# A third feed-forward by seven block products, and the forget-gate sums made one stage later

## The chip, the core and the metric

The kernel runs on one core of a Trainium2 chip. The core has a matrix engine (PE, with its weight loads shown apart as PEld), three engines for element-wise work (DVE, ACT, POOL) and a queue engine (SP) that issues most transfers; POOL issues some. The metric is the device time of one execution in microseconds, smaller is better. One execution was also recorded by the hardware profiler; all rows below come from that record.

## What is computed

The reference is one inference step of a two-layer decoder for 512 prompt tokens and 32 sample tokens (8 sequences of 4), all in float32. Each layer is: feed-forward, mixer, feed-forward. So there are four feed-forwards; the mixer of the first layer is a gated linear attention, that of the second a "forgetting" attention over shared keys and values.

```python
def swiglu(u, w_up, w_down):              # u: 544 x 1024, w_up: 1024 x 5632, w_down: 2816 x 1024
    a, b = jnp.split(u @ w_up, 2, axis=-1)
    return (jax.nn.silu(a) * b) @ w_down
...
logf = jax.nn.log_sigmoid((fl + b_f).astype(jnp.float32))      # one value per token and head
Ft = jnp.cumsum(logf.astype(jnp.float32), axis=1)              # enters the scores as Fi - Ft
...
h = h + 0.5 * gate * swiglu(u, ...)       # u = modulate(rmsnorm(h)), before and after each mixer
```

## The kernel before

**Layout.** Activations are kept transposed: 1024 features are 8 blocks (`NB`) of 128 partitions, the 544 tokens are two halves of 272 columns (`HALF`). Every float32 operand of a large product is split into a high and a low part (`halves`, lines 156 to 158: ACT rounds the high part, DVE subtracts to get the low part), and each product is three matmuls (`acc3`, lines 173 to 178). One feed-forward has 22 pairs (`NQ`): pair q is 128 columns of `a` and the 128 columns of `b` that gate them.

**The plain feed-forward, `ffn` (line 412).** For each pair and each half of the tokens, `up` makes `a` and `b`, each with 8 x 3 matmuls of 272 columns: 96 matmuls for a pair. `gated` (line 442 on) applies SiLU, multiplies and splits the result into `gh`, `gl`. `down` multiplies groups of pairs (2, 4, 4, 4, 4, 4) by the rows of `w_down` and `residual` (line 389) adds to `h`. In the last group all eight blocks of half 0 come first, then all eight of half 1; behind each half come `stats` and `make_u`, which make the input of the next stage. The plain form was used for three feed-forwards, named "00", "02" and "10"; their matmuls write tiles `pa`, `pb` and `pd`.

**The feed-forward by seven products, `ffn_seven` (line 508).** It was used for the last one alone, "12". The first three pairs are done plainly (`plain`). From the fourth pair on, the 2 x 2 blocks of the weights (a or b, by halves of the features) and of the inputs (by halves of the features and of the tokens) are multiplied by a scheme of seven block products in place of eight: 7 x 4 x 3 = 84 matmuls for a pair, which write tiles `p`. The block sums that it needs are extra work: of the inputs once (`inputs`, `last_input`: tiles `x`, `t`, `th`, `tl`), of the weights for each pair (`stage`: POOL, lines 611 to 618, and `halves`), of the results for each pair (`plus_ps`, line 643, and `low`, lines 648 and 649). `T3`, a block of the inputs, is written over a quarter of `uh`/`ul`. The 16 blocks of `down` of a round (rounds of 3, 3, 3, 3, 3, 3, 2, 2 pairs) are issued between the products of the next round; the last round, of two pairs, has half 0 first, then half 1.

**The forget gates' sums.** Four functions, `gate_logs`, `gate_turn`, `gate_tiles`, `gate_pages` (lines 1478 to 1523), turn the raw gate values `lf` into what the attention reads: rows of the DRAM scratch `klscr` and `qxscr`, and the tiles `nf` and `cum`. In the kernel before they are passed as `steps` to feed-forward "10" (line 1528), which issues one after every eleventh `gated`. Their tiles lie in a pool of their own, opened before "10".

**The attention, `fox` (line 1533 on).** After "10" come the projections `fq` (queries, two chunks of 512 columns, with `norm_heads` on DVE and POOL), then eight blocks `og_block` (`fg`, 48 matmuls each), whose weights come through `split_cols` and SP. The attention proper starts with the `cq` products and with `pair_loads(0)`, which reads `khscr`, `klscr` and `qxscr` back by POOL's queue into `kd`, `kl` and `qe`; the first score products `fs` need all three.

**The order of the work.** The kernel is written for a framework that schedules each engine's instructions itself: an instruction goes to its engine's queue when, by the framework's own estimate, its inputs and its tile's memory are there, and what stands earlier in the program goes first among those that are ready. So an instruction can run well ahead of the place where it is written. `gate_logs`, written behind the eleventh `gated` of "10", ran at the very start of "10"; the POOL memset of `gate_turn` and the 16 page loads of `gate_pages` ran before "10" began. Rings of buffers set limits: 4 raw weight tiles, 6 high, 6 low, 5 product banks.

Of the kernel before, what the change touches and what calls it, by code (L numbers as in the profile page):

```python
# [9 lines left out]
F32 = mybir.dt.float32  # L10
# [8 lines left out]
P = 128  # L19
# [80 lines left out]
def trunk_kernel(ctx: ExitStack, tc: tile.TileContext, a, out, dbg=None, stop=None):  # L100
# [407 lines left out]
    def ffn_seven(name, l, s, gate, after_half, steps=(), final=False, plain=3):  # L508
        wu = a["w_ffn_up"][l, s]
        wd = a["w_ffn_down"][l, s]  # L510
        steps = list(steps)
# [6 lines left out]
        with tc.tile_pool(name="ffn" + name, bufs=1) as fp:  # L518
            th, tl = ({i: fp.tile([P, H2, HA], F32R, name=f"t{x}{i}{name}") for i in (1, 2, 4)} for x in "hl")
            t3 = fp.tile([P, H2, HA], F32, name=f"t3{name}")  # L520
# [14 lines left out]

            def inputs():
                for k in range(H2):
                    x1, x2 = (tmp.tile([P, HA], F32, tag="nv", name=f"x{i}{name}_{k}", bufs=3)[:] for i in (1, 2))
                    x3 = t3[:, k]
# [6 lines left out]
                    minus(x3, x2, x3)  # L546
                    minus(x2, x2, x1)
                    halves(th[2][:, k], tl[2][:, k], x2)
                    x4 = tmp.tile([P, HA], F32, tag="nv", name=f"x4{name}_{k}", bufs=3)[:]
                    plus(x4, 1, 0, k)  # L550
                    minus(x4, x4, x2)
                    halves(th[4][:, k], tl[4][:, k], x4)
                    yield

            def last_input():
                S.copy(quarter(uh, 0, 1), t3[:])
                minus(quarter(ul, 0, 1), t3[:], quarter(uh, 0, 1).bitcast(F32))
# [8 lines left out]
            def g_tiles(q):  # L566
                gt[q] = (fp.tile([P, T], F32R, tag="gh", name=f"gh{name}_{q}", bufs=6),
                         fp.tile([P, T], F32R, tag="gl", name=f"gl{name}_{q}", bufs=6))
# [8 lines left out]
            def plain_up(q, half):  # L577
                t0, t1 = HALF[half]
# [3 lines left out]
                apply_u(pb, wt[q][1], half)  # L582
                g = tmp.tile([P, HA], F32, tag="sq", name=f"g{name}_{q}_{half}", bufs=3)
                S.activation(g[:], pa[:, 0:HA], AF.Silu)
                V.tensor_tensor(out=g[:], in0=g[:], in1=pb[:, 0:HA], op=ALU.mult)
                halves(gt[q][0][:, t0:t1], gt[q][1][:, t0:t1], g[:])

# [63 lines left out]
            def seven(q, between):  # L651
# [32 lines left out]
                if steps:  # L684
                    steps.pop(0)()
# [34 lines left out]
            for q in range(2):  # L720
                plain_weights(q)
            plain_up(0, 0)
            plain_up(1, 0)
            plain_up(0, 1)
# [21 lines left out]
            for r in range(1, len(rounds)):  # L746
                todo = blocks(r - 1)
                n, done = 7 * len(rounds[r]), [0]

                def between():  # L750
                    done[0] += 1
                    while len_out[0] < 2 * NB * done[0] // n:
                        next(todo)
                        len_out[0] += 1
                len_out = [0]
# [658 lines left out]
    gates = ExitStack()  # L1414
    gt_pool = gates.enter_context(tc.tile_pool(name="gate", bufs=1))
    lf = gt_pool.tile([P, 5, 16], F32, name="lf")
# [50 lines left out]
    le = gt_pool.tile([P, 5, 16], F32, name="le")  # L1467
    lt = gt_pool.tile([16, TP], F32, name="lt")
    rs = gt_pool.tile([16, TP], F32, name="rs")
    loc = gt_pool.tile([16, TP], F32, name="loc")  # L1470
    loc2 = gt_pool.tile([16, 2, TP], F32R, name="loc2")
    off = gt_pool.tile([16, 4, 4, 1], F32, name="off")
    off2 = gt_pool.tile([16, 2, 16], F32R, name="off2")
    gsm = gt_pool.tile([16, 16, P], F32, name="gsm")
    lp = gt_pool.tile([P, 2, 8, 16], F32, name="lp")
    lne = gt_pool.tile([32, 8, 16], F32, name="lne")

    def gate_logs():
        S.activation(le[:], lf[:], AF.Abs)
        S.activation(le[:], le[:], AF.Exp, scale=-1.0)  # L1480
        S.activation(le[:], le[:], AF.Ln, bias=1.0)
        V.tensor_scalar(out=lf[:], in0=lf[:], scalar1=0.0, scalar2=None, op0=ALU.min)
        V.tensor_tensor(out=lf[:], in0=lf[:], in1=le[:], op=ALU.subtract)
        G.dma_start(out=out[5][0].rearrange("(t p) h -> p t h", p=P), in_=lf[:, 0:4])
        G.dma_start(out=out[9].rearrange("b t h -> (b t) h"), in_=lf[0:32, 4])

    def gate_turn():
        ps = aux_bank("lfT")
        for t in range(4):
            PE.transpose(ps[0:16, t * P:(t + 1) * P], lf[:, t], ident)  # L1490
        V.tensor_copy(out=lt[:], in_=ps[0:16, :])
        G.memset(rs[:], 1.0)
        G.memset(rs[:].rearrange("p (c t) -> p c t", t=P)[:, :, 0:1], 0.0)
        V.tensor_tensor_scan(out=loc[:], data0=rs[:], data1=lt[:], initial=0.0, op0=ALU.mult, op1=ALU.add)

    def gate_tiles():
        hi, lo = loc2[:, 0], loc2[:, 1]
        halves(hi, lo, loc[:])
        SP.dma_start(out=klscr[:, 64:66], in_=loc2[:].bitcast(F32))
        V.memset(off[:], 0.0)  # L1500
        for qt in range(1, 4):
            for kt in range(qt - 1, -1, -1):
                V.tensor_tensor(out=off[:, kt, qt], in0=off[:, kt + 1, qt], in1=loc[:, kt * P + 127:kt * P + 128], op=ALU.subtract)
        halves(off2[:, 0], off2[:, 1], off[:].rearrange("p k q o -> p (k q o)"))
        for i in range(2):
            V.tensor_copy(out=gsm[:], in_=off2[:, i].bitcast(F32).unsqueeze(2).to_broadcast([16, 16, P]))
            SP.dma_start(out=qxscr[:, 2 + 4 * i:6 + 4 * i].rearrange("p k t -> p (k t)"), in_=gsm[:].rearrange("p a t -> p (a t)"))

    def gate_pages():
        for b in range(8):  # L1510
            for g in range(2):
                SP.dma_start(out=lp[:, g, b], in_=a["cache_logf"][bass.ds(pages[2 * b + g], 1)].rearrange("o t h -> t (o h)"))
        V.tensor_tensor(out=lne[:], in0=lf[0:32, 4].unsqueeze(1).to_broadcast([32, 8, 16]), in1=cst[0:32, C_SEQ:C_SEQ + 8].unsqueeze(2).to_broadcast([32, 8, 16]), op=ALU.mult)
        ps = aux_bank("nf")
        lpf = [lp[:, g].rearrange("p b h -> p (b h)") for g in range(2)]
        strict = cst[:, C_STRICT:C_STRICT + 128]
        PE.matmul(ps[:, 0:128], lhsT=lpf[0], rhs=strict, start=True, stop=False)
        PE.matmul(ps[:, 0:128], lhsT=lpf[1], rhs=ones, start=False, stop=True)
        PE.matmul(ps[:, 128:256], lhsT=lpf[1], rhs=strict, start=True, stop=True)
        PE.matmul(ps[:, 256:260], lhsT=lne[:].rearrange("p b h -> p (b h)"), rhs=cst[0:32, C_TRI4:C_TRI4 + 4], start=True, stop=True)  # L1520
        V.tensor_copy(out=nf[:, 0:256], in_=ps[:, 0:256])
        V.tensor_copy(out=cum[:], in_=ps[:, 256:260])
        V.tensor_scalar(out=nf[:, 256:260], in0=ps[:, 256:260], scalar1=-1.0, scalar2=None, op0=ALU.mult)
# [4 lines left out]
    ffn("10", 1, 0, mod(1, 0, 2), after("11", mod(1, 1, 0), mod(1, 1, 1)), [gate_logs, gate_turn, gate_tiles, gate_pages])  # L1528
    gates.close()
# [3 lines left out]
    def fox(after_half):  # L1533
        W = a["fox_w_qg"][0]
        with ExitStack() as es:
# [13 lines left out]
            with tc.tile_pool(name="foxq", bufs=1) as gp:  # L1549
# [293 lines left out]
```

## Time and profile before

| what | us |
|---|---|
| median of 3 runs | 2429.81 |
| fastest, slowest | 2422.88, 2434.22 |
| the profiled execution | 2429.69 |
| its span, first to last instruction | 2427.9 |
| feed-forward "10", first to last product | 1329.66 to 1733.00 |
| projections of the attention (`fq`, then `fg`) | 1734.81 to 1839.8 |
| feed-forward "12", first to last product | 2037.41 to 2419.95 |

Times in rows are microseconds from the start of the span. A row of the view by windows gives, for a stretch, each engine's busy time and the number of instructions that fall in it. A row of the view by lines gives a group of like instructions: line, engine, operation, out<-in, shape, count, then busy time and mean duration in ns, then the idle time of the engine before them and what ended it. Matmuls overlap each other, so that a matmul of "289 ns" does not cost the engine 289 ns; the cost of one is taken from how many start in a stretch that is full.

### The profile page before, as it was taken

To read this page: it belongs to the slowest core of one execution; us is meant where nothing else is said; L and a number is where in the kernel's file an instruction comes from. 1 tells how busy PE (TensorE), PEld (TensorE's weight loads), DVE (VectorE), ACT (ScalarE), POOL (GpSimd) and SP (SyncE) were. 2 spreads that over 40 slices of the span, in tenths; PEclk is the share of its full clock that TensorE was granted. 3 is DMA by queue.
4 is the path that set the end of the run, shared out by engine and by line. 5 is a ranking of instruction groups with operands and counts; after the bars stand their busy time and mean duration, and the time that the engine had idled before them with its cause. 6 is when DMAs were issued, how large, how long until landed. Compare 5 with 4: busy or idle time off the path is not lost.

```text
span 2427.9 us, 48518 instructions
## 1 busy us (share of the span) xinstructions
PE 2362.8 (97%) x19976; PEld 2215.4 (91%) x19976; DVE 1381.7 (57%) x3082; ACT 832.4 (34%) x1529; POOL 443.5 (18%) x574
## 2 busy tenths in 40 slices
PE   7999999998999999999999999999998899999999
PEld 6999999997979999999979999999896569999999
DVE  6343343548556453443585345344766666888887
ACT  3212222334534222221334323222435544444432
POOL 0000000206202010100120000000224212355442
PEclk8999999998999999999999999999999999999999
DMA  9636444322262645446337423222136751233322
GB/s 304 213 124 220 163 159 155 111 60 63 60 191 88 216 158 187 167 152 207 131 116 226 120 70 110 88 87 88 44 88 160 189 166 53 77 94 96 98 86 77
DMA packets 334131, 319.40 MB, mean 132 GB/s; under 512 B 24767, under 2 KB 287773, under 8 KB 333862
## 3 DMA queue, kind: packets, MB, share of 16 engines
q1 hardware_dynamic: 320134, 304.44, 39.5%
q0 software_dynamic: 13776, 11.87, 2.3%
q8 instruction: 157, 2.57, 0.4%
q14 instruction: 64, 0.52, 0.1%
HBM read 298.17 MB, written 18.38 MB: 130 GB/s over the span
## 4 chain that ended last, share of the span: by engine, by line
PE 82%; DVE 9%; DMA 4%; ACT 2%; POOL 2%; issue 1%; SPq 0%; ACTq 0%; DVEq 0%; POOLq 0%
PE pd L178 7%; PE pd L176 7%; PE pd L177 7%; PE pa L176 6%; PE pb L178 5%; PE pb L177 5%; PE pa L177 5%; PE pa L178 5%; PE pb L176 5%; PE p L177 3%; PE p L178 3%; PE p L176 3%; PE ada L231 3%; DMA kd<-khscr 2%; DVE nv L367 1%
## 5 line engine op out<-in xcount | busy, mean ns | idle before, releaser
L176 PE MATMUL pa<-uh,hua 128*128 128x272 f32 x1104 | 323.0, 293 | 1.8 <-ACT uh L386 1.7
L177 PE MATMUL pa<-ul,hua 128*128 128x272 f32 x1104 | 321.3, 291 | 0.4 <-DVE ul L387 0.2
L178 PE MATMUL pa<-uh,lua 128*128 128x272 f32 x1104 | 320.0, 290 | 0.0
L178 PE MATMUL pb<-uh,lub 128*128 128x272 f32 x1104 | 319.3, 289 | 0.0
L177 PE MATMUL pb<-ul,hub 128*128 128x272 f32 x1104 | 318.8, 289 | 0.0
L176 PE MATMUL pb<-uh,hub 128*128 128x272 f32 x1104 | 318.3, 288 | 0.0
L393 DVE SCALAR_TENSOR_TENSOR h<-pd,mods,h 128x272 f32<-128x272 f32 (+1 forms) x416 | 199.7, 481 | 194.8 <-PE pd L178 193.9
L178 PE MATMUL pd<-gh,lwd 128*128 128x272 f32 x1056 | 305.1, 289 | 0.0
L176 PE MATMUL pd<-gh,hwd 128*128 128x272 f32 x1056 | 305.0, 289 | 0.0
L177 PE MATMUL pd<-gl,hwd 128*128 128x272 f32 x1056 | 304.8, 289 | 0.0
L398 POOL TENSOR_TENSOR h<-h,gs 128x32 f32<-128x32 f32 x208 | 81.3, 391 | 941.4 <-DVE gs L396 936.0
L176 PEld LDWEIGHTS pa<-uh,hua 128*128 128x128 f32 x1104 | 208.9, 189 | 14.6 <-issue 6.0
L177 PEld LDWEIGHTS pa<-ul,hua 128*128 128x128 f32 x1104 | 209.3, 190 | 1.7 <-DVE ul L387 1.4
L178 PEld LDWEIGHTS pa<-uh,lua 128*128 128x128 f32 x1104 | 209.0, 189 | 0.0
L177 PEld LDWEIGHTS pb<-ul,hub 128*128 128x128 f32 x1104 | 209.0, 189 | 0.0
L176 PEld LDWEIGHTS pb<-uh,hub 128*128 128x128 f32 x1104 | 208.9, 189 | 0.0
L178 PEld LDWEIGHTS pb<-uh,lub 128*128 128x128 f32 x1104 | 208.7, 189 | 0.0
L446 DVE TENSOR_TENSOR g<-g,pb 128x272 f32<-128x272 f32 x132 | 57.7, 437 | 262.8 <-PE pb L178 261.4
L176 PEld LDWEIGHTS pd<-gh,hwd 128*128 128x128 f32 x1056 | 199.4, 189 | 1.7 <-issue 1.6
L177 PEld LDWEIGHTS pd<-gl,hwd 128*128 128x128 f32 x1056 | 199.3, 189 | 0.0
L178 PEld LDWEIGHTS pd<-gh,lwd 128*128 128x128 f32 x1056 | 199.1, 189 | 0.0
L157 ACT CAST hua<-rua 128x1024 fp32r<-128x1024 f32 x69 | 72.3, 1048 | 355.7 <-PE pd L177 264.2
(551 smaller groups left out, 5822.5 us busy)
## 6 DMA issues: line engine op xcount, KB each, us to landing
adaw<-in_w_ada_dram SPq DMA_DIRECT2D x128, 512.0 KB, 5.9
rua<-in_w_ffn_up_dram SPq DMA_DIRECT2D x88, 512.0 KB, 3.9
rub<-in_w_ffn_up_dram SPq DMA_DIRECT2D x88, 512.0 KB, 4.3
rwd<-in_w_ffn_down_dram SPq DMA_DIRECT2D x66, 512.0 KB, 5.0
rd<-in_w_ffn_down_dram SPq DMA_DIRECT2D x24, 384.0 KB, 3.3
adah<-in_w_ada_dram SPq DMA_DIRECT2D x16, 512.0 KB, 7.7
adaw<-in_w_ada_kv_dram SPq DMA_DIRECT2D x16, 512.0 KB, 6.4
s<-in_state_gla_dram SPq DMA_DIRECT2D x16, 512.0 KB, 4.4
```

The lines of the kernel that those rows point to most:

```text
L157: S.copy(hi, src)
L176: PE.matmul(ps, lhsT=wh, rhs=xh, start=first and i == 0, stop=False)
L177: PE.matmul(ps, lhsT=wh, rhs=xl, start=False, stop=False)
L178: PE.matmul(ps, lhsT=wl, rhs=xh, start=False, stop=last and i == n - 1)
L231: PE.matmul(ps[32 * j:32 * j + 32, 0:256], lhsT=sc[:, k, :], rhs=t[:, j * 256:(j + 1) * 256], start=k == 0, stop=k == NB - 1)
L367: V.scalar_tensor_tensor(out=v[:, 0:p1 - t0], in0=h[:, k, t0:p1], scalar=mods[:, scale + k, 0:1], in1=rb[:, t0:p1], op0=ALU.mult, op1=ALU. ...
L393: V.scalar_tensor_tensor(out=h[:, m, t0:p1], in0=ps[:, 0:n], scalar=mods[:, gate + m, 0:1], in1=h[:, m, t0:p1], op0=ALU.mult, op1=ALU.add)
L398: G.tensor_tensor(out=h[:, m, TP:T], in0=h[:, m, TP:T], in1=st[:], op=ALU.add)
L446: V.tensor_tensor(out=g[:], in0=g[:], in1=pb[:, 0:HA], op=ALU.mult)
```

## The change

1. Feed-forward "10" calls `ffn_seven` instead of `ffn`. Its first three pairs stay plain and 19 of its 22 go by seven products. "00" and "02" stay plain, "12" stays as it was.
2. The four gate functions, and the page loads as a fifth, are no longer `steps` of "10". They are made by `gate_work(pool)` and issued one behind each of the first five `og_block`s of the attention's projections. Their tiles lie in the pool `foxq`, which is opened after "10"; `lf` itself moves to a pool that lives on.
3. `ffn_seven` gets what `ffn` had for work between its parts: the pieces that `after_half(0)` returns (the eight `make_u` of half 0) are now issued one by one behind the last round's blocks of half 1, from the third on. Its new arguments `first`, `held`, `slots` and `late` have their defaults in both calls, which leaves those branches out; with `slots=6` the pacing of the rounds is what it was.

```diff
-    ffn("10", 1, 0, mod(1, 0, 2), after("11", mod(1, 1, 0), mod(1, 1, 1)), [gate_logs, gate_turn, gate_tiles, gate_pages])
-    gates.close()
+    ffn_seven("10", 1, 0, mod(1, 0, 2), after("11", mod(1, 1, 0), mod(1, 1, 1)))
...
             r = len(rounds) - 1
+            us_ = []
             for half in range(2):
                 for m in range(NB):
                     down_block(r, m, half, True)
-                    if half == 0 and m % 2 == 0:
-                        down_weights(r, m // 2 + 1) if m < NB - 2 else None
-                after_half(half)
+                    if half == 0 and m % 2 == 0 and m < NB - 2:
+                        down_weights(r, m // 2 + 1)
+                    if half and m >= 2 and us_:
+                        us_.pop(0)()
+                if held:
+                    held.pop(0)()
+                while us_:
+                    us_.pop(0)()
+                us_ = after_half(half) or []
...
-    lf = gt_pool.tile([P, 5, 16], F32, name="lf")
+    lf = kvp.tile([P, 5, 16], F32, name="lf")
...
+    def gate_work(pool):
+        le = pool.tile([P, 5, 16], F32, name="le")
...
+        def gate_loads():
+            for b in range(8):
+                for g in range(2):
+                    SP.dma_start(out=lp[:, g, b], in_=a["cache_logf"][bass.ds(pages[2 * b + g], 1)].rearrange("o t h -> t (o h)"))
...
+        return [gate_loads, gate_logs, gate_turn, gate_tiles, gate_pages]
...
                 left = proj_tokens("fq", W, [[(0, 512)], [(512, 512)]], evac_fq, evac_fqs)
+                gates = gate_work(gp)
                 for i in range(NB):
                     og_block(i)
                     if left:
                         left.pop(0)()
+                    if gates:
+                        gates.pop(0)()
```

The bodies of the gate functions are as before, but that the page loads are taken out of `gate_pages`. What is left out of the diff is the branches that neither call takes and the same change of pool for the other gate tiles.

More of the change, by code (lines that the diff above doesn't have):

```diff
@@ L503, in ffn, with ffn_seven, tick @@
                 s_()
-    def ffn_seven(name, l, s, gate, after_half, steps=(), final=False, plain=3):
+    def ffn_seven(name, l, s, gate, after_half, steps=(), final=False, first=None, held=(), slots=6, late=False):
         wu = a["w_ffn_up"][l, s]
         wd = a["w_ffn_down"][l, s]
-        steps = list(steps)
+        steps, held = list(steps), list(held)
+        plain = 3
+        total, ticks, n_ticks = len(steps), [0], 2 * plain + 7 * (NQ - plain)
+        def tick():
+            ticks[0] += 1
+            for _ in range(total * ticks[0] // n_ticks - (total - len(steps))):
+                steps.pop(0)()
         rounds, q0 = [], 0
@@ L519, in ffn_seven @@
             th, tl = ({i: fp.tile([P, H2, HA], F32R, name=f"t{x}{i}{name}") for i in (1, 2, 4)} for x in "hl")
-            t3 = fp.tile([P, H2, HA], F32, name=f"t3{name}")
+            t3 = None if late else fp.tile([P, H2, HA], F32, name=f"t3{name}")
             gt, ops, raws, down_w = {}, {}, {}, {}
@@ L534, in plus, with short @@
                 V.tensor_tensor(out=dst, in0=x, in1=y, op=ALU.add)
+            def short(what, k):
+                return tmp.tile([P, HA], F32, tag="nv", name=f"x{what}{name}_{k}", bufs=3)[:]
             def inputs():
                 for k in range(H2):
-                    x1, x2 = (tmp.tile([P, HA], F32, tag="nv", name=f"x{i}{name}_{k}", bufs=3)[:] for i in (1, 2))
-                    x3 = t3[:, k]
+                    x1, x2, x3 = short(1, k), short(2, k), short(3, k) if late else t3[:, k]
                     plus(x3, 0, 1, k)
@@ L545, in inputs @@
                     plus(x2, 1, 1, k)
-                    minus(x3, x2, x3)
+                    if not late:
+                        minus(x3, x2, x3)
                     minus(x2, x2, x1)
                     halves(th[2][:, k], tl[2][:, k], x2)
-                    x4 = tmp.tile([P, HA], F32, tag="nv", name=f"x4{name}_{k}", bufs=3)[:]
+                    x4 = short(4, k)
                     plus(x4, 1, 0, k)
@@ L555, in last_input @@
             def last_input():
-                S.copy(quarter(uh, 0, 1), t3[:])
-                minus(quarter(ul, 0, 1), t3[:], quarter(uh, 0, 1).bitcast(F32))
+                if not late:
+                    S.copy(quarter(uh, 0, 1), t3[:])
+                    minus(quarter(ul, 0, 1), t3[:], quarter(uh, 0, 1).bitcast(F32))
+                    return
+                for k in range(H2):
+                    x2, x3 = short(5, k), short(6, k)
+                    plus(x2, 1, 1, k)
+                    plus(x3, 0, 1, k)
+                    minus(x2, x2, x3)
+                    t0, t1 = HALF[1]
+                    halves(uh[:, k, t0:t1], ul[:, k, t0:t1], x2)
             def operand(i, kh=0, half=0):
@@ L566, in g_tiles @@
             def g_tiles(q):
-                gt[q] = (fp.tile([P, T], F32R, tag="gh", name=f"gh{name}_{q}", bufs=6),
-                         fp.tile([P, T], F32R, tag="gl", name=f"gl{name}_{q}", bufs=6))
+                gt[q] = (fp.tile([P, T], F32R, tag="gh", name=f"gh{name}_{q}", bufs=slots),
+                         fp.tile([P, T], F32R, tag="gl", name=f"gl{name}_{q}", bufs=slots))
             wt = {}
@@ L577, in plain_up @@
             def plain_up(q, half):
-                t0, t1 = HALF[half]
                 pa = mm_bank(f"pa{name}_{q}_{half}")
@@ L582, in plain_up, with gated @@
                 apply_u(pb, wt[q][1], half)
+                gated(q, half, pa, pb)
+            def gated(q, half, pa, pb):
+                t0, t1 = HALF[half]
                 g = tmp.tile([P, HA], F32, tag="sq", name=f"g{name}_{q}_{half}", bufs=3)
@@ L586, in plain_up @@
                 halves(gt[q][0][:, t0:t1], gt[q][1][:, t0:t1], g[:])
+                tick()
             W4 = H2 * P
@@ L718, in blocks, with part_of_bank @@
                         yield
[L720 to L724, printed above, removed]
+            if first:
+                wt[0], feed = first
+                g_tiles(0)
+                banks = [[mm_bank(f"p{x}{name}_0_{half}") for x in "ab"] for half in range(2)]
+                def part_of_bank(half, part):
+                    for i in range(2):
+                        apply_u(banks[half][i], wt[0][i], half, 4 * part, 4 * part + 4)
+                part_of_bank(0, 0)
+                ready = feed()
+                with tc.issue_after(ready):
+                    part_of_bank(1, 0)
+                for half in range(2):
+                    part_of_bank(half, 1)
+                for half in range(2):
+                    gated(0, half, *banks[half])
+                plain_weights(1)
+                plain_up(1, 0)
+            else:
+                for q in range(2):
+                    plain_weights(q)
+                plain_up(0, 0)
+                plain_up(1, 0)
+                plain_up(0, 1)
             t_ops = inputs()
@@ L747, in ffn_seven @@
                 todo = blocks(r - 1)
-                n, done = 7 * len(rounds[r]), [0]
+                n, done, gone = min(7 * len(rounds[r]), 7 * (slots - 3)), [0], [0]
                 def between():
                     done[0] += 1
-                    while len_out[0] < 2 * NB * done[0] // n:
+                    while gone[0] < min(2 * NB * done[0] // n, 2 * NB):
                         next(todo)
-                        len_out[0] += 1
-                len_out = [0]
+                        gone[0] += 1
+                    tick()
                 for q in rounds[r]:
@@ L1466, in trunk_kernel @@
             G.dma_start(out=vs_out[:, 256 * j:256 * j + 256], in_=vnew[32 * j:32 * j + 32, :])
[L1467 to L1507, printed above, removed]
```

68 lines of the change are left out of this document (49 added, 19 removed).

## The prediction, made before the result was known

> **What bounds the kernel now.** I read the page first, for the engine that is never free.
>
> ```profile
> span 2427.9 us, 48518 instructions
> PE 2362.8 (97%) x19976; PEld 2215.4 (91%) x19976; DVE 1381.7 (57%) x3082; ACT 832.4 (34%) x1529; POOL 443.5 (18%) x574
> PE 82%; DVE 9%; DMA 4%; ACT 2%; POOL 2%; issue 1%; SPq 0%; ACTq 0%; DVEq 0%; POOLq 0%
> ```
>
> PE is busy for 97% of the span and makes up 82% of the chain that ended last. So taking matmuls away should pay, wherever PE has no gaps and nothing else is late next. That is a question for each stage; the view by windows answers it. Its rows are, in order: the middle of feed-forward "10" (plain), the middle of "12" (seven products), most of "12", the seam from the last blocks of "10" into the `fq` projections, its second part, and the `fg` projections.
>
> ```profile
> core 0: us, PE busy (x) PEld busy (x) DVE busy (x) ACT busy (x) POOL busy (x), PEclk, DMA share, GB/s
> 1360.00:1700.00 340.00, 340.00 (x2705) 339.91 (x2704) 147.00 (x266) 85.67 (x135) 14.75 (x40) 1.00 0.29 89
> 2100.00:2400.00 300.00, 298.82 (x2381) 298.60 (x2380) 249.87 (x433) 121.21 (x203) 146.29 (x152) 1.00 0.31 93
> 2056.00:2414.00 358.00, 354.16 (x2800) 353.01 (x2801) 302.47 (x540) 143.18 (x247) 161.42 (x164) 1.00 0.28 83
> 1717.60:1786.00 68.40, 66.79 (x475) 56.97 (x474) 60.67 (x213) 27.95 (x51) 20.23 (x26) 1.00 0.22 70
> 1733.10:1786.00 52.90, 51.47 (x354) 42.05 (x353) 49.00 (x175) 23.14 (x40) 15.01 (x17) 1.00 0.29 91
> 1786.00:1838.00 52.00, 51.63 (x405) 50.92 (x404) 18.20 (x56) 18.64 (x40) 10.98 (x11) 1.00 0.46 94
> ```
>
> Three things are to be seen. "10" is bound by PE alone: 340.00 of 340.00, with DVE at 43%. "12" is what "10" is to become: PE still has 298.82 of 300, but DVE has 83% (249.87), so the cover is there and not large. And the seam behind "10" is full on two engines at once: DVE has 60.67 of 68.4 us there, 49.00 of 52.90 in its second part. The clock is 1.00 throughout.
>
> **The gross gain.** The counts of the groups confirm how many matmuls a form takes.
>
> ```profile
> L176 PE MATMUL pa<-uh,hua 128*128 128x272 f32 x1104 | 323.0, 293 | 1.8 <-ACT uh L386 1.7
> L176 PE MATMUL pd<-gh,hwd 128*128 128x272 f32 x1056 | 305.0, 289 | 0.0
> ```
> ```profile
> L176 PE MATMUL p<-uh,hu 128*128 128x272 f32 x304 | 88.2, 290 | 0.0
> L176 PE MATMUL p<-th,hu 128*128 128x272 f32 x228 | 65.8, 289 | 1.8 <-ACT th L157 1.8
> L177 PE MATMUL pd<-gl,hd 128*128 128x272 f32 x346 | 100.1, 289 | 1.2 <-POOL gl L649 1.2
> ```
>
> A plain feed-forward has 22 x 96 = 2112 matmuls for `a` and `b` and, from 1056 for three feed-forwards and three such lines, 1056 of `pd`: 3168. "12" has (304 + 228) x 3 = 1596 for 19 pairs (84 each), 3 x 96 = 288 for the plain ones, and 1056 of `pd`: 2940. So "10" loses 228, as 19 x 12 says. One costs 340 / 2705 = 0.1257 us in "10" and 300 / 2381 = 0.1260 us in "12"; the difference holds the small waits of the seven-product form (the 1.2 us on `gl` in the row above among them). 3168 x 0.1257 = 398.2 against 2940 x 0.1260 = 370.4: **27.8 us less**. The rest of the new work (block sums on POOL, DVE, ACT, two more rounds of `residual`) lies under PE by the measured row of "12", which has all of it; if that cover were gone, DVE's 302.47 of 358 says that it would take 18% more DVE work.
>
> A row of this form is the slow DVE product `c`: line 680 against the same shape at line 446 of the plain form.
>
> ```profile
> L680 DVE TENSOR_TENSOR c<-c,c 128x272 f32<-128x272 f32 x19 | 18.2, 956 | 0.0
> ```
> ```profile
> L446 DVE TENSOR_TENSOR g<-g,pb 128x272 f32<-128x272 f32 x44 | 19.3, 438 | 79.0 <-PE pb L178 78.8
> ```
>
> 956 against 438 ns: DVE is held up while POOL works. The Trainium skill ("SBUF — State Buffer", section "Who interferes with whom") has a rule that speaks against this change: a DVE instruction with two inputs in SBUF and a POOL instruction that reads SBUF share a port as a lock, and the later one waits for the whole of the other. The rows agree in kind, 518 ns on 19 such products. In the sum this is already paid: DVE's 302.47 us of "12" contain the waits. The rival that would follow is worked out below.
>
> **The start of "10": 0.3 us (0 to 1.8).** "12" has a wait before its first products, 1.8 us until `th` in the row above, because DVE came late out of `make_u`.
>
> ```profile
> 2057.68 0.76 DVE ul L387 x2
> ```
> ```profile
> 1333.27 0.85 DVE L387 SCALAR_TENSOR_TENSOR ul<-nv,mods,uh 128x240 fp32r<-128x240 f32 x2
> ```
> ```profile
> 2037.41 0.37 PE L176 MATMUL pa<-uh,hua 128*128 128x272 f32 x1
> ```
> ```profile
> 1329.66 0.29 PE L176 MATMUL pa<-uh,hua 128*128 128x272 f32 x1
> ```
>
> There the last `ul` ended at 2058.4, in "10" at 1334.1. The first product of "12" began at 2037.4, that of "10" at 1329.7: DVE is free 21.0 us behind PE's start in the one and 4.4 in the other, a lead of 16.6 us against a wait of 1.8. Weight splits that "12" had done by then still follow in "10" and use a part of the lead. So I take little.
>
> **The end of "10": 5.5 us (0 to 7.7).** This is the largest unknown. No run shows a seven-product form with `make_u` behind it. In the kernel before the last group has four pairs, so the eight blocks of half 1 are 96 matmuls, 12.1 us of PE, under which DVE takes half 0 through `stats` and `make_u`. Now the last round has two pairs: 48 matmuls, 6.0 us.
>
> ```profile
> 1733.00 0.29 PE L178 MATMUL pd<-gh,lwd 128*128 128x272 f32 x1
> 1734.57 0.38 PE L359 MATMUL st<-cst,sq 128*128 128x1 f32 x2 [1.28 <-POOL sq L350]
> ```
> ```profile
> 1720.95 0.16 DVE L328 TENSOR_SCALAR nx<-st 128x3 f32<-128x3 f32 x1 [2.52 <-PE st L359]
> 1726.26 1.92 DVE L367 SCALAR_TENSOR_TENSOR nv<-h,mods,rb 128x272 f32<-128x272 f32 x3 [0.44 <-ACT rb L339]
> 1738.26 0.49 DVE L387 SCALAR_TENSOR_TENSOR ul<-nv,mods,uh 128x272 fp32r<-128x272 f32 x1
> ```
>
> DVE starts on half 0's statistics at 1720.95, has the scale at 1726.26, and ends half 0's `ul` at 1738.75, 5.7 us after PE's last block. This chain doesn't get shorter. PE would now reach `fq` 6 us sooner and find fewer `ul` ready. At best (0) it walks through `fq` block by block as they come; at worst all that the shorter round saves, 6.0, is spent waiting. DVE has 68.4 - 60.67 = 7.7 us free in this seam; 6 us less time would leave 1.7. With 97% asked of it, I take three quarters of the worst, 4.5. A wait can also cost the clock, as at the seam in front of "12".
>
> ```profile
> 2037.00:2042.00 5.00, 4.13 (x33) 3.91 (x33) 4.40 (x9) 2.43 (x5) 0.44 (x1) 1.00 0.35 96
> 2042.00:2045.50 3.50, 3.50 (x18) 3.50 (x19) 3.23 (x5) 1.54 (x2) 2.47 (x2) 0.53 0.73 210
> ```
>
> The rows are two stretches there. PE stood idle for 0.87 of 5 us around half 1's statistics, and behind it the granted clock is 0.53 for 3.5 us: 18 matmuls where 28 would fit, some 1.7 us lost at half speed. That goes on top of the worst (7.7), and with somewhat more than half its weight on what I take: 5.5. The Trainium skill ("TensorE: Matmul & The Clock Gate", section "Part 1: The HAM clock gate (the "warmup" mystery)") lets the clock fall after an idle window of about 3.4 us; by that rule alone waits as short as these would cost no clock and this term would be 4.5, the time 1 us less. The rows differ, with 0.87 us idle in front of the fall, and they decide.
>
> **The gate functions: 1 us (-1.5 to 5.0).** They leave "10" and come into the projections with every instruction.
>
> ```profile
> L1490 PE MATMUL lfT<-cst,lf x4: 270/272/273, 1498.7 to 1499.1; 128*16 128x128 f32 x4
> L1491 DVE COPY lt<-lfT x1: 679/679/679, 1499.4 to 1499.4; 16x512 f32<-16x512 f32 x1
> ```
> ```profile
> L1494 DVE TENSOR_TENSOR_SCAN loc<-rs,lt x1: 1205/1205/1205, 1501.5 to 1501.5; 16x512 f32<-16x512 f32 x1
> ```
> ```profile
> L1506 DVE COPY gsm<-off x2: 1207/1208/1210, 1504.1 to 1510.5; 16x2048 f32<-16x2048 f32 x2
> L1507 SPq DMA_DIRECT2D qxscr<-gsm x2: 308/320/331, 1505.3 to 1511.8; - x2
> DMA to landing us min/median/max: 3.1/3.1/3.1
> ```
> ```profile
> L1512 SPq DMA_DIRECT2D lp<-in_cache_logf_dram x16: 332/333/413, 1231.5 to 1253.2; - x16
> ```
> ```profile
> 1749.72 2.67 SPq L876 DMA_DIRECT2D rfq<-in_fox_w_qg_dram  x4
> 1774.99 28.96 SPq L163 DMA_DIRECT2D rfg<-in_fox_w_qg_dram  x8
> ```
>
> PE's own share (4 transposes and 8 small products: at 0.1257 us each 1.5 us, an estimate) only moves, and could fall into a gap of the seam: that is the -1.5. DVE's larger instructions are 0.7 + 1.2 + 2 x 1.2 = 4.3 us, and with the like of `lt` once more for the split of `loc`, 5.0. In the `fg` stretch DVE has 34 of 52 us free and they cost nothing; in the `fq` stretch, where 3.9 are free, they would be in the way: that is the 5.0. Written behind `fg` blocks they are last in rank there, so I take 1. On SP's queue the 16 page loads (16 x 0.33 = 5.3 us) pass the `rfg` weight loads; SP is idle from 1752.4 to 1775.0, and even 5.3 us in front of `rfg` would meet weights a block ahead. Two stores on POOL's queue move along and meet nothing urgent. New waits stand behind the scratch rows: POOL's queue can load `qe` only when both `qxscr` stores have landed, and the next loads of `kl` and `kd` queue behind it.
>
> **The sum.** 27.8 - 0.3 - 5.5 - 1 = 21.0 us, off the profiled execution's own 2429.69 (its span of 2427.9 and 1.8 around it; the median, 2429.81, is the same): **2409 us**, rounded up. With the ends of the three unknowns: 29.3 to 13.3 us, 2400 to 2416.
>
> **Rivals.** *The seam eats half (0.20).* DVE becomes the bound from the last round to the end of `fq`, and the gate work lands in it: 7.7 + 5.0 + 1.8 = 14.5 us lost, 13.3 gained, 2416. For it: 49.00 of 52.90. Against: DVE has slack right behind, and the framework ranks the work.
>
> *The gate chain comes too late (0.08).* From the first transpose to the second store's landing the chain took 1511.8 + 3.1 - 1498.7 = 16.2 us; then `qe` has to load, and the scores need it.
>
> ```profile
> L1701 POOL DMA_DIRECT2D qe<-qxscr x8: 567/588/616, 1817.8 to 1940.9; - x8
> DMA to landing us min/median/max: 7.1/12.3/15.5
> ```
> ```profile
> 1839.80 0.48 PE L1722 MATMUL fs<-kd,uh 128*128 128x512 f32 x1
> ```
>
> So 28.5 us stand between the transposes and `fs` at 1839.8: the chain decides from 1811.3 on (clock of before). `gate_turn` is written behind the third of eight blocks, 1786 + 3 x 6.5 = 1805.5, which leaves 5.8 us. If the framework lets the transposes slip behind all eight, to 1838, the attention starts 26.7 us late: 2409 + 27 = 2436, slower than before. Against: PE takes in program order what is ready, and `lf` is ready long before.
>
> *It doesn't arrive (0.08).* The 228 matmuls go, but waits on DVE, the weight loads or the rings fill the room: 2427. Against: "12" doesn't show it.
>
> *The lock decides (0.03).* If each us of POOL held DVE on top of what it shows, DVE would need 302.47 + 161.42 = 463.9 us where "10" takes 403.3 (1329.7 to 1733.0): 61 us slower, 2490. "12" ran in 358 with both. By the skill's page this is the rule's limit; the trace doesn't agree with that much.
>
> **The numbers.** The forecast has 0.61. The range is 2400 to 2424: from the lower end of the sum over the half-eaten seam at 2416, and some 7 us on, since the three runs before lie up to 7 us from their median. It holds the forecast and the first rival, 0.81, and leaves the others out. About 0.5%, 12 us, is what a measurement of this kernel can tell from no change: faster by more means below 2417.7. That is the forecast and some 0.12 of the first rival, which lies close to the bound: 0.73. Within it lie the rest of that rival (0.08), the gain that doesn't arrive (0.08) and most of the late chain (0.06): 0.22. Slower: the lock and a still later chain, 0.05.
>
> **What would show it.** Right: `p` with 1064 x 3 matmuls, "10" some 376 us from first to last product, about 0.126 us each; DVE near 83% in it; a gap of PE of some us between the last `pd` of "10" and `fq`; `lfT` between `fg` blocks or earlier, and `fs` waiting for no load. Wrong: gaps among the products, `fs` waiting for `qe`, or `fq` stretched by DVE beyond 6 us.

## The result and the profile after

| | kernel before | changed kernel |
|---|---|---|
| median of 4 runs, us | 2428.97 (2422.88 to 2434.22) | 2411.99 (2408.00 to 2416.72) |
| profiled run, us | 2429.69 | 2416.72 |
| its span, us | 2427.9 | 2414.6 |

The ratio is 0.9932 with a 95% interval of 0.9902 to 0.9961, that is 9.5 to 23.8 us saved, 17.0 by the medians. The forecast was 2409 us, 21 saved. The profiled run is the slowest of the four, 13.0 us faster than the profiled run of before; the difference is worked out by stages below. Three single runs far off all others (9112, 4403 and 2535 us), met in the experiments, are left out of every median, ratio and interval.

Three lines of the profile's page, after:

```profile
span 2414.6 us, 48788 instructions
PE 2340.1 (97%) x19748; PEld 2188.1 (91%) x19748; DVE 1528.2 (63%) x3341; ACT 881.3 (36%) x1627; POOL 595.4 (25%) x700
PE 38%; DVE 4%; DMA 4%; POOL 1%; ACT 1%; issue 1%; SPq 0%; POOLq 0%; DVEq 0%; ACTq 0%
```

The last line is the chain that ended last, by engine. Its shares add up to 49% here and to 100% before, so PE's share in the one isn't held against the other. PE has exactly 228 matmuls fewer (19976 - 19748), DVE 259 instructions and POOL 126 more. PE is busy for 22.7 us less, not for 27.8. The groups of `p` in the view by instruction, which lists the first and last start, show that "10" has the new form: 608 + 456 = 1064 of each of the three products.

```profile
L176 PE MATMUL p<-uh,hu x608: 282/288/297, 1365.0 to 2391.3; 128*128 128x272 f32 x152
L176 PE MATMUL p<-th,hu x456: 282/288/394, 1366.5 to 2389.0; 128*128 128x272 f32 x152
```

Now the whole stretch which the change touches on PE, from the first `pa` of "10" to the first `fg`. This is the view by windows; its columns are those of the prediction's first rows. First before:

```profile
1329.70:1788.50 458.80, 457.19 (x3569) 446.65 (x3568) 233.43 (x535) 136.62 (x225) 40.16 (x73) 1.00 0.29 88
```

and after, with the middle of "10" and with the stretches around its end:

```profile
1328.80:1769.60 440.80, 433.47 (x3331) 421.18 (x3330) 374.30 (x781) 186.14 (x324) 193.69 (x202) 0.98 0.31 92
1400.00:1670.00 270.00, 269.31 (x2145) 269.08 (x2144) 226.88 (x384) 109.39 (x182) 138.45 (x141) 1.00 0.31 93
1699.00:1702.40 3.40, 3.40 (x16) 3.40 (x16) 2.03 (x12) 1.48 (x3) 1.37 (x4) 0.50 0.00 0
1702.40:1709.20 6.80, 3.70 (x27) 3.19 (x25) 6.43 (x20) 3.58 (x9) 6.27 (x12) 1.00 0.31 80
1709.20:1713.90 4.70, 3.85 (x18) 3.85 (x19) 2.52 (x6) 3.56 (x7) 1.74 (x3) 0.50 0.17 16
1713.90:1719.50 5.60, 5.60 (x14) 4.44 (x15) 5.57 (x22) 2.28 (x5) 0.37 (x1) 0.50 0.04 5
```

The stretch is 18.0 us shorter (458.80 - 440.80). The body of "10" is as forecast: 270 / 2145 = 0.1259 us each, with DVE at 84%. The loss sits at the seam, and it has two parts. PE is idle for 7.33 us of the stretch (440.80 - 433.47), where it was idle for 1.61 before; and between 1699.0 and 1719.5 the granted clock is 0.50 in two stretches, of 3.4 us and of 4.7 + 5.6 = 10.3 us (the rows split the second where `fq` begins), 13.7 us in all. The timeline of PE shows what it waited for (a bracket is the idle time before the row and what ended it):

```profile
1694.48 0.29 PE L178 MATMUL pd<-gh,ld 128*128 128x272 f32 x1
1696.30 0.38 PE L359 MATMUL st<-cst,sq 128*128 128x1 f32 x2 [1.53 <-POOL sq L350]
...
1697.35 1.62 PE L359 MATMUL st<-cst,sq 128*128 128x1 f32 x14
...
1704.70 0.29 PE L178 MATMUL pd<-gh,ld 128*128 128x272 f32 x1
1706.99 1.12 PE L337 MATMUL rb<-diag,cst 128*128 128x128 f32 x6 [2.00 <-DVE diag L336]
1710.05 4.02 PE L359 MATMUL st<-cst,sq 128*128 128x1 f32 x18 [1.94 <-POOL sq L350]
1713.93 0.77 PE L967 MATMUL fq<-hfq,uh 128*128 128x512 f32 x1
```

Three waits of 1.5 to 2.0 us stand there: half 0's squares from POOL, its scale (`diag`) from DVE, and half 1's squares from POOL. The first `fq` starts 9.2 us after the last `pd`; before it was 1.8 (1733.00 to 1734.81). And 18 statistics products, which before lay among the `fq`, now stand ahead of them and take 4.02 us at half clock.

POOL's timeline says why half 0's squares were late:

```profile
1691.23 5.01 POOL L350 TENSOR_TENSOR sq<-sq,sq 128x272 f32<-128x272 f32 x5 [1.31 <-ACT sq L346]
```

Five square sums run back to back, 1.0 us each. A block of a round with two pairs is 2 x 3 = 6 matmuls, 0.75 us of PE. So PE hands out blocks faster than POOL squares them here. With four pairs a block takes 1.5 us.

The stages of the two profiled runs, from the first and last starts on PE:

| stage, us | before | after | change |
|---|---|---|---|
| up to the first `pa` of "10" | 1329.7 | 1328.8 | -0.9 |
| "10", first `pa` to last `pd` | 403.3 | 375.9 | -27.4 |
| last `pd` to first `fq` | 1.8 | 9.2 | +7.4 |
| `fq` to first `fg` | 53.7 | 55.7 | +2.0 |
| `fg` to first `fs` | 51.2 | 52.2 | +1.0 |
| attention, `fs` to last `fo` | 143.4 | 147.3 | +3.9 |
| from there to the end of the span | 444.7 | 445.5 | +0.8 |

The 3.9 us of the attention are no part of this change as far as the runs show: over all nine kernels below and above, this stage took 141.7 to 148.2 us with the same work in it, 143.4 before and 148.2 in a kernel that saves nothing. The part ahead of "10" scatters in the same way, 1328.4 to 1335.2 us. This scatter is as large as the terms that I was after; so the experiments are read first by the stretch from `pa` to `fg`, and their times second.

### The profile page after: what moved, and what is told of

It is laid out like the page before. It is cut to its first block, busy times and chain, and to the rows that moved or that the text cites. A ratio compares the mean times of both kernels' runs of the same rounds, so it can differ in the third digit from the quotient of the medians.

```text
span 2414.6 us, 48788 instructions
## 1 busy us (share of the span) xinstructions
PE 2340.1 (97%) x19748; PEld 2188.1 (91%) x19748; DVE 1528.2 (63%) x3341; ACT 881.3 (36%) x1627; POOL 595.4 (25%) x700
## 5 line engine op out<-in xcount | busy, mean ns | idle before, releaser
L178 PE MATMUL pa<-uh,lua 128*128 128x272 f32 x800 | 231.3, 289 | 0.0
L177 PE MATMUL pd<-gl,hd 128*128 128x272 f32 x704 | 204.0, 290 | 2.1 <-POOL gl L672 2.1
L178 PE MATMUL pd<-gh,ld 128*128 128x272 f32 x704 | 204.0, 290 | 0.2 <-DVE ld L158 0.2
L176 PE MATMUL pd<-gh,hd 128*128 128x272 f32 x704 | 203.5, 289 | 0.0
L178 PE MATMUL pd<-gh,lwd 128*128 128x272 f32 x704 | 203.3, 289 | 0.0
L176 PE MATMUL pd<-gh,hwd 128*128 128x272 f32 x704 | 203.2, 289 | 0.0
L177 PE MATMUL pd<-gl,hwd 128*128 128x272 f32 x704 | 202.5, 288 | 0.0
L178 PE MATMUL p<-uh,lu 128*128 128x272 f32 x608 | 175.5, 289 | 0.0
L176 PE MATMUL p<-uh,hu 128*128 128x272 f32 x608 | 175.0, 288 | 0.0
L177 PE MATMUL p<-ul,hu 128*128 128x272 f32 x608 | 175.0, 288 | 0.0
L176 PEld LDWEIGHTS pa<-uh,hua 128*128 128x128 f32 x800 | 151.1, 189 | 14.8 <-issue 6.0
```

The lines of the kernel that those rows point to most:

```text
L176: PE.matmul(ps, lhsT=wh, rhs=xh, start=first and i == 0, stop=False)
L177: PE.matmul(ps, lhsT=wh, rhs=xl, start=False, stop=False)
L178: PE.matmul(ps, lhsT=wl, rhs=xh, start=False, stop=last and i == n - 1)
```

## The experiments

Four theories stood against each other for the loss at the seam. **Cover**: the last round's two pairs are too short to hide half 0's statistics and scale. **Gates**: the moved gate functions are pulled into the seam (the trace of after has their two ACT table loads at 1705.68 and 1710.88, between `pd` and `fq`) and delay the scale. Their lines in ACT's timeline:

```profile
1705.68 1.28 ACT L1526 ACT_TABLE_LOAD   x1
1710.88 1.28 ACT L1527 ACT_TABLE_LOAD   x1
```

**Rounds**: it is the number of rounds, not the size of the last. **Scatter**: there is no loss beyond the noise.

**The changed kernel again.** No edit.

> The changed kernel once more, for its spread and as the measure of the other runs. Two theories of why 17 us came and not 21. Cover: the shorter last round leaves PE waiting for half 0's statistics and make_u, and the wait brings the half clock. Gates: the gate functions were pulled forward into the seam behind feed-forward 10, and their two table loads (1.28 us each) on ACT and the memset on POOL hold up make_u and the statistics. Both expect 2412 here, 9.2 us from the last pd to the first fq, and the attention from the first fs to the last fo within 3 us of the kernel before; if that stretch is again 3.8 us longer than before, the move of the gates has a cost there as well.

Measured: 2413.83 us (6 runs) against 2429.00 (17 runs), ratio 0.9933 (0.9916 to 0.9950), so 12 to 20 us saved; the gap is 9.1 us again and the seam has 13.6 us at half clock. From the first `pa` to the first `fg` it takes 440.5 us, where the first profile had 440.8. The loss is not scatter. The attention takes 144.6 us here, 1.2 more than before, so its 3.9 us did not come again.

**The gate functions alone.**

```diff
-    ffn_seven("10", 1, 0, mod(1, 0, 2), after("11", mod(1, 1, 0), mod(1, 1, 1)))
+    ffn("10", 1, 0, mod(1, 0, 2), after("11", mod(1, 1, 0), mod(1, 1, 1)))
```

> Feed-forward 10 plain again, the gate functions still in the projections. Cover: the seam is as in the kernel before, 1.8 us from the last pd to the first fq, fq 53 us, and the time is that of before within 2 us. Gates: the table loads and the memset land in this seam too and cost here also, the seam 2 to 4 us longer, the time 2 to 4 us above before.

Measured: 2432.27 us (11 runs), ratio 1.0006 (0.9996 to 1.0017): from 1 us saved to 4 us lost, which fits either theory. Its seam in PE's timeline:

```profile
1733.65 0.29 PE L178 MATMUL pd<-gh,lwd 128*128 128x272 f32 x1
1735.22 0.38 PE L359 MATMUL st<-cst,sq 128*128 128x1 f32 x2 [1.27 <-POOL sq L350]
1735.46 0.48 PE L967 MATMUL fq<-hfq,uh 128*128 128x512 f32 x1
```

The gap is 1.8 us as before, and the first `fg` comes 457.6 us after the first `pa`, 1.2 less than before: PE's own share of the gate work has left "10". Moved behind a plain "10", the gate functions do nothing to the seam. Their two table loads start 3.3 us behind the first `fq` in this run, though (1738.72 and 1740.31), and not ahead of it; so it doesn't settle the theory of the gates by itself, and the next run has to.

**The gate functions held back**, with the seven products, so that neither ACT nor POOL can take them up before the `fg` blocks' own work. (`behind["pool"]` is set in the same way, to the last product of `norm_heads` on POOL.)

```diff
-                        S.activation(sg[i // 2][:, i % 2, t0:p1], ps[:, 0:p1 - t0], AF.Sigmoid)
+                        behind["act"] = S.activation(sg[i // 2][:, i % 2, t0:p1], ps[:, 0:p1 - t0], AF.Sigmoid)
...
-                        gates.pop(0)()
+                        with tc.issue_after(behind["act"].ins), tc.issue_after(behind["pool"].ins):
+                            gates.pop(0)()
```

> The changed kernel, but the ACT and POOL instructions of the gate functions are tied behind the sigmoid of the fg block they are written after and behind the last norm product on POOL, so that they can't go into the seam. Cover: at most 1 us better than the changed kernel, the seam stays at 8 to 9 us. Gates: uh no longer waits for table loads, the seam shrinks by 3 to 5 us and with it the half clock, 2407 to 2409.

Measured: 2414.59 us (7 runs), ratio 0.9948 (0.9928 to 0.9967). ACT's timeline has the two table loads far behind the seam now, and PE's timeline has the seam unchanged:

```profile
1784.73 1.28 ACT L1528 ACT_TABLE_LOAD   x1
1786.31 1.28 ACT L1529 ACT_TABLE_LOAD   x1
```
```profile
1705.40 0.29 PE L178 MATMUL pd<-gh,ld 128*128 128x272 f32 x1
1707.92 0.85 PE L337 MATMUL rb<-diag,cst 128*128 128x128 f32 x6 [2.23 <-DVE diag L336]
1710.53 4.42 PE L359 MATMUL st<-cst,sq 128*128 128x1 f32 x18 [1.76 <-POOL sq L350]
1714.81 0.77 PE L967 MATMUL fq<-hfq,uh 128*128 128x512 f32 x1
```

The gap is 9.4 us, and the stretch from `pa` to `fg` takes 440.5 us. The theory of the gates falls: what ACT and POOL did for the gates in the seam cost nothing. (SP's 16 page loads were not held back and still run from 1706.8 to 1714.5; no wait of PE in the seam ended on them.)

**Four pairs in the last round.** `ffn_seven` gets an argument `sizes`, which stands in place of the tuple of rounds; "10" passes another, "12" the old one.

```diff
-        for n in (3, 3, 3, 3, 3, 3, 2, 2):
+        for n in sizes:
...
+    ffn_seven("10", 1, 0, mod(1, 0, 2), after("11", mod(1, 1, 0), mod(1, 1, 1)), sizes=(3, 3, 3, 3, 3, 3, 4))
```

> The changed kernel with rounds of 3, 3, 3, 3, 3, 3, 4 pairs in feed-forward 10, so that half 1's last blocks are again 96 matmuls, 12.1 us of cover. Cover: from the last pd to the first fq some 3 us, fq back to 53 us, 2404 to 2407. Gates: the table loads are still in the seam, so the seam keeps most of its length, 7 us or more, 2410 to 2412.

Measured: 2402.28 us (5 runs, 2401.41 to 2404.47), ratio 0.9892 (0.9876 to 0.9907): 23 to 30 us saved. Its stretch and the seam's windows, then the seam in PE's timeline:

```profile
1332.00:1760.80 428.80, 426.69 (x3331) 416.02 (x3330) 371.19 (x757) 184.86 (x319) 185.39 (x189) 1.00 0.31 95
1705.20:1712.20 7.00, 5.50 (x35) 4.69 (x33) 5.53 (x16) 6.06 (x12) 3.68 (x9) 1.00 0.34 83
```
```profile
1705.11 0.28 PE L178 MATMUL pd<-gh,ld 128*128 128x272 f32 x1
1706.90 0.38 PE L359 MATMUL st<-cst,sq 128*128 128x1 f32 x2 [1.50 <-POOL sq L350]
1707.14 0.48 PE L967 MATMUL fq<-hfq,uh 128*128 128x512 f32 x1
...
1710.71 1.51 PE L359 MATMUL st<-cst,sq 128*128 128x1 f32 x13
```

This is the seam of before again, one wait of 1.5 us behind the last `pd`, with `fq` at full clock and the statistics of half 1 among them. The gap is 2.0 us; gap and time are a little better than the theory of the cover said. Against the changed kernel, with the same 3331 recorded matmuls, the stretch is 12.0 us shorter. The two rows split this: 5.2 us less idle time (7.33 against 2.11) and 6.8 us less busy time (433.47 against 426.69). Most of the 6.8 is the clock. At 0.50 a product of 272 columns takes 0.227 us (13 of them take from 1699.07 to 1702.02 in the changed kernel) and not 0.126, so the 12.9 busy us at half clock hold some 7.1 us of work, and some 5.7 are lost (an estimate). The rows don't say what the last 1.1 us are.

**Three pairs in the last round**: `sizes=(3, 2, 2, 3, 3, 3, 3, 3)` in the same place.

> The changed kernel with rounds of 3, 2, 2, 3, 3, 3, 3, 3 pairs in feed-forward 10: eight rounds as in the changed kernel, but 72 matmuls, 9.1 us, in half 1's last blocks. If the cover of half 1 sets the seam, it lies between two pairs (gap 9.2 us, fq 55.8) and four (2.0 and 53.7): a gap of 3 to 6 us, 2404 to 2409. If four pairs helped because there was one round less, nothing changes: gap 9 us, 2411 to 2414.

Measured: 2409.48 us (5 runs, 2405.85 to 2417.11), ratio 0.9924 (0.9902 to 0.9946). The stretch lies between the two:

```profile
1335.20:1768.20 433.00, 427.76 (x3331) 415.62 (x3330) 375.31 (x781) 184.68 (x321) 192.43 (x199) 1.00 0.31 94
```

```profile
1709.56 0.29 PE L178 MATMUL pd<-gh,ld 128*128 128x272 f32 x1
1710.77 0.51 PE L967 MATMUL fq<-hfq,uh 128*128 128x512 f32 x1 [0.92 <-ACT uh L386]
1728.40 0.86 PE L955 MATMUL fq_s<-rfq,us 128*32 128x128 f32 x24 [1.85 <-POOL us L378]
```

The gap is 1.2 us, less than the 3 to 6 expected; `fq` takes 57.4 us instead, longer than with two pairs, as waits that stood in the gap now stand among `fq`. PE is idle for 5.2 us, in small waits, the longest of 1.85 us ahead of `fq_s`, and the clock stays at 1.00. By the stretch three pairs give back 7.8 of the 12.0 us. By the time nothing can be told from the changed kernel: the intervals lie on each other, and in the profiled run the part ahead of "10" happened to be 6.4 us longer.

**Two pairs last, but seven rounds**: `sizes=(3, 3, 3, 3, 4, 4, 2)`.

> Rounds of 3, 3, 3, 3, 4, 4, 2 pairs in feed-forward 10: seven rounds like the run with four pairs last, but again two pairs last. Cover: the gap stays at 9 us and fq at 55 to 56, with the half clock, 2409 to 2413; one round less is worth 0 to 2 us in feed-forward 10. Number of rounds: gap 2 to 3 us, 2402 to 2405.

Measured: 2413.85 us (4 runs), ratio 0.9936 (0.9912 to 0.9960).

```profile
1712.24 0.29 PE L178 MATMUL pd<-gh,ld 128*128 128x272 f32 x1
1714.03 0.85 PE L337 MATMUL rb<-diag,cst 128*128 128x128 f32 x6 [1.50 <-DVE diag L336]
1717.55 4.00 PE L359 MATMUL st<-cst,sq 128*128 128x1 f32 x18 [2.67 <-POOL sq L350]
1721.41 0.77 PE L967 MATMUL fq<-hfq,uh 128*128 128x512 f32 x1
```

The gap is 9.2 us, with 6.8 us at half clock ahead of it and 10.2 from within it on; the stretch takes 442.6 us. It is the size of the last round, not the number of rounds.

**Work put in to no end.** Behind each block of half 1 in the last round of "10" the products of that block are made once more, into a bank that nobody reads: 48 matmuls, the 6.0 us by which the last round is shorter than a four-pair one. Nothing is left out.

```diff
+                    if half and not final:
+                        wh, wl = down_w[r, m // 2]
+                        c = slice((m % 2) * P, (m % 2) * P + P)
+                        t0, t1 = HALF[half]
+                        acc3(mm_bank(f"fill{m}")[:, 0:HA], [(wh[:, i, c], wl[:, i, c], gt[q][0][:, t0:t1], gt[q][1][:, t0:t1]) for i, q in enumerate(rounds[r])])
```

> The changed kernel with 48 more matmuls in the last round of feed-forward 10: each block of half 1 is followed by the same six matmuls into a bank that nobody reads (work added, nothing left out). It asks what PE's time is worth there. Cover with the clock: PE only filled its own wait; the 6.0 us cost nothing, and where they keep the clock at full speed they even pay: gap 2 to 4 us, no half clock in the seam, 2408 to 2413. If PE had no time to spare there: 6 us slower, 2418 to 2420.

Measured: 2412.14 us (4 runs), ratio 0.9927 (0.9903 to 0.9951), the time of the changed kernel. The windows of its stretch and PE's timeline at its seam:

```profile
1333.70:1773.00 439.30, 435.83 (x3378) 425.19 (x3377) 376.82 (x781) 186.03 (x323) 194.02 (x201) 0.99 0.30 92
```
```profile
1717.84 0.29 PE L178 MATMUL fill<-gh,ld 128*128 128x272 f32 x1
1718.71 0.38 PE L359 MATMUL st<-cst,sq 128*128 128x1 f32 x2 [0.58 <-POOL sq L350]
1719.58 0.38 PE L359 MATMUL st<-cst,sq 128*128 128x1 f32 x2 [0.49 <-ACT sq L346]
1719.83 0.48 PE L972 MATMUL fq<-hfq,uh 128*128 128x512 f32 x1
```

PE does 6 us more work and the stretch is 1.5 us shorter. Useless work fitted where PE had only waited, and from the last `pd` on the clock stayed at 1.00. Ahead of that the expectation missed: the wait for half 0's squares is 1.53 us as in the changed kernel, and 6.8 us went by at half clock behind it, among half 1's filled blocks; in the changed kernel it was 3.4.

```profile
1702.80:1709.60 6.80, 6.80 (x32) 6.80 (x32) 3.21 (x19) 1.38 (x2) 1.11 (x3) 0.50 0.00 0
```

**Four pairs last in both feed-forwards.** As above, and "12" gets the same sizes.

> Four pairs in the last round in feed-forward 12 as well as in 10. Behind 12 there is only the store, no make_u, so no cover is missing: cover expects no more than what one round less gives, 0 to 2 us against 2402.3, 2400 to 2403; a gain of 5 us or more would say that four pairs help by something else.

Measured: 2400.56 us (4 runs, 2398.91 to 2403.99), ratio 0.9887 (0.9862 to 0.9912): 21 to 34 us faster than the kernel before. "12" took 379.3 us from first `pa` to last `pd` against 381.4 with two pairs last, and the seam of "10" is that of the four-pair kernel. Whether the 1.7 us between the two medians are real can't be told, the intervals overlap; it is the best median of all kernels here.

## Why the prediction was right, and which term was off

The total came out within 4 us by the medians, the signs and the mechanism held, and one term was mis-sized by 6.5 us, more than the total is off. That the total is off by less is luck as far as the runs can tell: the interval of what was saved is 14 us wide.

- **Gross gain, 27.8: right.** "10" takes 376 us as said. Cleanest is the four-pair kernel, whose seam costs nothing new: its stretch is 30.0 us shorter than before, of which some 1.5 is PE's share of the gate work gone elsewhere, which leaves 28.5. That the block sums would lie under PE was right too: 269.31 of 270 us.
- **Start of "10", 0.3: it was 0.** The group by lines of the first `p` from `th` shows no idle time ahead of any of its 228 in "10":

```profile
L176 PE MATMUL p<-th,hu 128*128 128x272 f32 x228 | 65.7, 288 | 0.0
```

- **End of "10", 5.5 (0 to 7.7): 12 by the stretch, 10 to 12 by the medians. This is the step that failed.** I had named the cause, the shorter cover, and split the term into "three quarters of the worst, 4.5" and a clock loss of about 1. The first part was nearly right: 5.7 us more idle time than before. The second was not: PE is busy for 6.8 us more than in the four-pair kernel, of which some 5.7 are the clock by the estimate above. I took the clock's price from the seam ahead of "12", one stretch of 3.5 us. (Its row has 18 matmuls where 28 would fit; the 10 that are missing are 1.3 us at 0.126 each, not the 1.7 that I took by the clock alone.) Here there are three waits and some 13.6 us at half clock. The worst case, "all that the shorter round saves", was no bound for the same reason: cover that is too short by 6 us can cost more than 6 us when the waits slow what comes after them. I also laid the wait on DVE alone. One of the three is DVE's: from 1702.4 to 1709.2 it is busy for 6.43 of 6.80 us, and the wait for `diag` ends on it. The other two ended on POOL's squares, and DVE is idle for 2.2 of the 4.7 us ahead of `fq`. It is a chain of ACT, POOL, PE and DVE steps that sets the pace there, not one full engine all through.
- **Gate functions, 1 (-1.5 to 5): right.** The `fg` stage is 1.0 us longer, and alone they cost -1 to 4. The transposes sit where I put them, behind the third `fg` block, and the first scores wait for nothing. (Later ones wait for `kd`, 12.2 us in all, against 11.3 before and 10.0 in the repetition.) But I had put all of this work last in rank, and its table loads on ACT, which I had given no price, its memset on POOL and its page loads on SP ran ahead of its place, in the seam. That they cost nothing there is shown for ACT and POOL by the run that holds them back. From the view by source line and PE's timeline:

```profile
L1536 PE MATMUL lfT<-cst,lf x4: 272/272/273, 1788.8 to 1789.1; 128*16 128x128 f32 x4
```
```profile
1821.02 0.95 PE L1634 MATMUL cq<-cum,cf 128*128 128x4 f32 x8
1821.83 0.48 PE L1773 MATMUL fs<-kd,uh 128*128 128x512 f32 x1
```

- **The rivals.** *The seam eats half* (14.5 us lost, 2416) is 4 us from the median of the result, the forecast 3; but of its parts only the seam itself counted, with DVE full in a part of it, and neither the start nor the gate work did. *The gate chain comes too late* falls by the two rows above, *it doesn't arrive* by the stretch's 18 us, *the lock decides* by the middle of "10": with DVE at 84% and POOL at 51% PE still had 269.31 of 270 us. The mean of 956 ns that I read hides two kinds. Of the 19 products `c` in "12" of the kernel before, nine took 0.44 us and ten 1.00 to 1.54. Each of the ten runs beside POOL products for nearly its whole length (the second below starts 0.08 us behind one of 1.31 us), and seven of the nine overlap none:

```profile
2200.81 0.44 DVE L680 TENSOR_TENSOR c<-c,c 128x272 f32<-128x272 f32 x1
2216.78 1.53 DVE L680 TENSOR_TENSOR c<-c,c 128x272 f32<-128x272 f32 x1
```

With the term as measured the sum is 27.8 - 0 - 12 - 1 = 14.8 us, inside the interval of what was saved in the run of the result (9.5 to 23.8) and in its repetition (12 to 20).

## What to carry to other kernels

When a stage gets cheaper on the engine that bounds it, look at the seam behind it: work that was hidden under its last round is still there, and the round that hides it has become shorter. Make the last round long enough to hide it: four pairs in place of two brought 10 to 12 us more here, on top of the change's 17. A first sign is to compare, per block, what the bounding engine needs (here 0.75 us) with what each engine in the chain behind it needs (POOL's 1.0 us); that comparison is read from one trace, and no run tried it by itself. Price a wait of the matrix engine with the clock that it may lose afterwards, not with its own length.

## What the runs showed of the hardware that I had not expected

- **Short waits can cost as much again by the clock.** In the seam after, around waits of 1.53, 2.00 and 1.94 us some 13.6 us went by at a granted clock of 0.50: some 5.7 us of lost work (the estimate above) for 5.5 us of waiting. A stretch at half clock lasted 3.4, 6.8 or some 10.2 us in these seams. The Trainium skill ("TensorE: Matmul & The Clock Gate", section "Part 1: The HAM clock gate (the "warmup" mystery)") lets it fall after an idle window of about 3.4 us; no single wait here was that long. What decides stays open: a wait of 1.50 us in the four-pair kernel and one of 1.27 in the kernel with the gates alone were followed by full clock, one of 1.53 here was not; with three pairs last, 5.2 us of waits up to 1.85 us cost no clock at all. Behind the one of 1.53 PE ran mainly statistics products of a single column; whether those count as idle was not tried.
- **A statistics product of one column still costs PE's time**: 14 of them took 1.62 us in a row at full clock, and 18 took 4.02 at 0.50.
- **The same code varies by several us from kernel to kernel, and the clock with it**: the attention stage by 6.5 us (141.7 to 148.2), the part ahead of "10" by 6.8. Over the ten profiles the attention takes 141.7 to 143.4 us in the five with a mean clock of 0.95 or 0.96 in this stage, 144.6 to 147.3 in the four with 0.94, and 148.2 in the one with 0.93. Whether the clock or the waits ahead of its fall come first is not shown. A single profiled run can't price a term of a few us by its total; a stretch between two marks can.
